# Short-sequence attention: 1 KB runs in DRAM, V reordered on TensorE, groups of 8 heads in three stages

## The chip, the core and the metric

The kernel runs on one core of a Trainium2 chip. The metric is device time in microseconds (us), the median of several runs. Beside those runs stands one profiled execution, from which every row below is taken. Engines: PE is TensorE (matmuls; PEld are its weight loads), DVE is VectorE, ACT is ScalarE, POOL is GpSimd, SP is SyncE. POOL issues the loads here and SP the stores; 16 DMA engines carry both. SBUF is the on-chip memory of 128 partitions, PSUM the memory of eight banks into which matmuls write.

## The reference

Attention for 32 batches of 12 heads, each with 128 tokens of 64 elements, no mask:

```python
scores = (1.0 / np.sqrt(64)) * np.matmul(q, k.transpose(0, 1, 3, 2))
attn = np.exp(scores - np.max(scores, axis=-1, keepdims=True))
attn = attn / (np.sum(attn, axis=-1, keepdims=True) + 1e-8)
return np.matmul(attn, v).astype(np.float32)
```

`q`, `k`, `v` and the result are float32 of shape (32, 12, 128, 64), 12.58 MB each. Both kernels compute in bf16 with float32 sums, leave the maximum out (the scores are small), and get the sum of each row of `attn` from a column of ones that stands beside V.

## The kernel before

The loop goes over the 32 batches. A batch is loaded by three DMAs on POOL's queue, which turn float32 into bf16 on the way (L52 q, L54 k, L57 v). A partition of SBUF holds one token, for all 12 heads, so that the runs in DRAM are the 64 floats of one token of one head: 256 B, and the same for the store. `v_bf` has 65 columns a head, the last set to one by a memset on POOL (L56). Input tiles have three buffers.

Then two heads at a time (`p` in 0 to 5): PE transposes 128 tokens x 128 elements of q into `qt_ps` (L63), ACT copies it to SBUF (L68), PE transposes the same of k into `kt_ps` (L70), DVE copies it (L75). `qt_ps` and `kt_ps` have one PSUM buffer each.

Then four heads at a time (`g` in 0 to 2): PE makes the four score matmuls into `sT_ps`, one bank a head (L84; a head's 64 elements lie in partitions 0 to 63 or 64 to 127, so neighbouring heads use the two halves of the array's rows). The scores come transposed, keys in the partitions. ACT takes the exp of all four (L92) into `attnT`. Two heads at a time, PE multiplies `attnT` with V and its ones into `o_ps` (L103), and DVE copies the two results to `o_b` (L110). `sT_ps` (four banks) and `o_ps` (two banks) have one buffer each.

At the end of a batch DVE takes the reciprocal of the 12 sums (L116), multiplies (L118), and SP issues the store (L119).

The instructions of an engine run in its own queue. The framework orders them by priority and by what is ready, within the buffers of each pool, and puts in the semaphores; a new tile of a pool waits until the reader of its old buffer has finished.

Of the kernel before, what the change touches and what calls it, by code (L numbers as in the profile page):

```python
# [1 line left out]

# [5 lines left out]


@with_exitstack
def kernel(
    ctx: ExitStack,
    tc: tile.TileContext,
    q: bass.AP,
    k: bass.AP,
    v: bass.AP,
    out: bass.AP,
):
    nc = tc.nc  # L20
    f32 = mybir.dt.float32
    bf16 = mybir.dt.bfloat16

    B, H, S, D = q.shape
    assert S == 128 and D == 64
    scale = 1.0 / (D ** 0.5)
    HT = 128 // D
    NP = H // HT
    HX = 4
    HO = 2  # L30
    BANK = 512

    qr = q.rearrange("b h s d -> b s h d")
    kr = k.rearrange("b h s d -> b s h d")
    vr = v.rearrange("b h s d -> b s h d")
    orr = out.rearrange("b h s d -> b s h d")

    singles = ctx.enter_context(tc.tile_pool(name="singles", bufs=1))
    ident = singles.tile([128, 128], bf16)
    make_identity(nc, ident)  # L40

    pbf = ctx.enter_context(tc.tile_pool(name="pbf", bufs=3))
    pt = ctx.enter_context(tc.tile_pool(name="pt", bufs=3))
    pa = ctx.enter_context(tc.tile_pool(name="pa", bufs=6))
    po = ctx.enter_context(tc.tile_pool(name="po", bufs=2))
    ps_t = ctx.enter_context(tc.tile_pool(name="ps_t", bufs=1, space=bass.MemoryType.PSUM))
    ps_s = ctx.enter_context(tc.tile_pool(name="ps_s", bufs=1, space=bass.MemoryType.PSUM))
    ps_o = ctx.enter_context(tc.tile_pool(name="ps_o", bufs=1, space=bass.MemoryType.PSUM))

    for b in range(B):  # L50
        q_bf = pbf.tile([128, H, D], bf16, tag="q_bf")
        nc.gpsimd.dma_start(out=q_bf, in_=qr[b])  # L52
        k_bf = pbf.tile([128, H, D], bf16, tag="k_bf")
        nc.gpsimd.dma_start(out=k_bf, in_=kr[b])  # L54
        v_bf = pbf.tile([128, H, D + 1], bf16, tag="v_bf")
        nc.gpsimd.memset(v_bf[:, :, D:D + 1], 1.0)  # L56
        nc.gpsimd.dma_start(out=v_bf[:, :, :D], in_=vr[b])  # L57

        qt = pt.tile([128, NP, 128], bf16, tag="qt")
        kt = pt.tile([128, NP, 128], bf16, tag="kt")  # L60
        for p in range(NP):
            qt_ps = ps_t.tile([128, 128], bf16, tag="qt_ps")
            nc.tensor.transpose(  # L63
                qt_ps,
                q_bf[:, p * HT:(p + 1) * HT, :].rearrange("a b c -> a (b c)"),
                ident,
            )
            nc.scalar.copy(qt[:, p, :], qt_ps)  # L68
            kt_ps = ps_t.tile([128, 128], bf16, tag="kt_ps")
            nc.tensor.transpose(  # L70
                kt_ps,
                k_bf[:, p * HT:(p + 1) * HT, :].rearrange("a b c -> a (b c)"),
                ident,
            )
            nc.vector.tensor_copy(kt[:, p, :], kt_ps)  # L75

        o_b = po.tile([128, H, D + 1], f32, tag="o_b")

        for g in range(H // HX):
            sT_ps = ps_s.tile([128, HX, BANK], f32, tag="sT")  # L80
            for i in range(HX):
                h = g * HX + i
                p, j = divmod(h, HT)
                nc.tensor.matmul(  # L84
                    sT_ps[:, i, :128],
                    lhsT=kt[j * D:(j + 1) * D, p, :],
                    rhs=qt[j * D:(j + 1) * D, p, :],
                    start=True,
                    stop=True,
                )  # L90
            attnT = pa.tile([128, HX, 128], bf16, tag="attnT")
            nc.scalar.activation(  # L92
                out=attnT,
                in_=sT_ps[:, :, :128],
                func=mybir.ActivationFunctionType.Exp,
                bias=0.0,
                scale=scale,
            )
            for gg in range(HX // HO):
                o_ps = ps_o.tile([128, HO, BANK], f32, tag="o_ps")  # L100
                for i in range(HO):
                    h = g * HX + gg * HO + i
                    nc.tensor.matmul(  # L103
                        o_ps[:, i, :D + 1],
                        lhsT=attnT[:, gg * HO + i, :],
                        rhs=v_bf[:, h, :],
                        start=True,
                        stop=True,
                    )
                nc.vector.tensor_copy(  # L110
                    o_b[:, g * HX + gg * HO:g * HX + (gg + 1) * HO, :],
                    o_ps[:, :, :D + 1],
                )

        recip = po.tile([128, H], f32, tag="recip")
        nc.vector.reciprocal(recip, o_b[:, :, D:D + 1])  # L116
        o_sb = po.tile([128, H, D], f32, tag="o_sb")
        nc.vector.tensor_mul(o_sb, o_b[:, :, :D], recip.to_broadcast([128, H, D]))  # L118
        nc.sync.dma_start(out=orr[b], in_=o_sb)  # L119


# [1 line left out]
_INS = ['q', 'k', 'v']  # L123
_OUTS = [((32, 12, 128, 64), 'float32')]


# [23 lines left out]
```

## Time and profile before

| | |
|---|---|
| time, median of 3 runs | 226.23 us (226.22 to 226.59) |
| span of the profiled execution | 224.4 us |
| PE busy | 168.3 us (75%), 1152 matmuls |
| PE weight loads busy | 83.1 us (37%), 1152 loads |
| DVE busy | 120.2 us (54%), 448 instructions |
| ACT busy | 99.7 us (44%), 289 instructions |
| POOL busy | 101.5 us (45%), 134 instructions |
| DMA packets | 198,674, of which 198,656 under 512 B |
| HBM traffic | 37.75 MB read, 12.58 MB written |

A row of groups reads: line, engine, operation, output <- input with shapes, count | busy us in total, mean ns of one | idle time of the engine just before them, and who ended it. A row of waits reads: who waited <- for whom: us in total, times, the longest. In the row of a stretch of time stand, after the stretch and its length, the busy time (and count) of PE, PEld, DVE, ACT and POOL, the granted clock of PE as a share, the summed time of packets as a share of 16 DMA engines, and GB/s. Packets of different queues overlap on an engine, so a sum of packet times can be over 100%. The bytes of a load count as they land, in bf16: half of what it reads.

### The profile page before, as it was taken

The page shows a single profiled execution, that of the slowest core. Times are in us where ns is not written, and L with a number is a line of the kernel's source. Part 1 is how long each engine was busy: PE and PEld are TensorE (multiplying, and loading weights), DVE is VectorE, ACT ScalarE, POOL GpSimd, SP SyncE. Part 2 cuts the span into 40 slices and gives each one's busy share as a digit, 9 for nine tenths or more (in the row PEclk, how much of TensorE's full clock was granted, in tenths as well). Part 3 has the DMA queues.
Part 4 walks back from the last instruction along what each step waited for, and adds up shares of the span by engine and source line. Part 5 has one row for each costly group of instructions (what it writes and reads, how often), then busy time and mean ns, then how long its engine had stood idle before and what let it go on. Part 6 is the DMA issues. An engine that isn't in the chain of part 4 may idle for free.

```text
span 224.4 us, 3513 instructions
## 1 busy us (share of the span) xinstructions
PE 168.3 (75%) x1152; PEld 83.1 (37%) x1152; DVE 120.2 (54%) x448; ACT 99.7 (44%) x289; POOL 101.5 (45%) x134
## 2 busy tenths in 40 slices
PE   0688787788787787877787877788877778878750
PEld 0344333344333343333343333444333334333330
DVE  0264555664555564555564555565555565456652
ACT  2554545445544445444445444444444444444320
POOL 8963455534475443455443455543355534222000
DMA  7999999999999999999999999999999999999333
GB/s 50 149 156 184 148 142 140 155 148 166 151 153 161 161 159 166 148 149 141 129 151 167 146 148 134 137 154 167 149 146 144 135 150 161 142 110 134 76 69 71
DMA packets 198674, 31.69 MB, mean 141 GB/s; under 512 B 198656, under 2 KB 198656, under 8 KB 198656
## 3 DMA queue, kind: packets, MB, share of 16 engines
q0 software_dynamic: 148992, 18.88, 131.9%
q1 hardware_dynamic: 49664, 12.58, 31.0%
q8 instruction: 9, 0.15, 0.3%
q14 instruction: 9, 0.07, 0.1%
HBM read 37.75 MB, written 12.58 MB: 224 GB/s over the span
## 4 chain that ended last, share of the span: by engine, by line
PE 64%; ACT 17%; DVE 9%; issue 6%; DMA 2%; ACTq 0%; POOL 0%; POOLq 0%
PE sT_ps L84 26%; PE qt_ps L63 14%; PE o_ps L103 14%; PE kt_ps L70 11%; ACT attnT L92 9%; ACT qt L68 7%; DVE o_b L110 5%; DVE kt L75 3%; DMA q_bf<-in_q_dram 2%; DVE o_sb L118 1%; ACTq L92 0%; DVE recip L116 0%; POOL ident masks.py:197 0%; POOLq masks.py:199 0%; POOLq L134 0%
## 5 line engine op out<-in xcount | busy, mean ns | idle before, releaser
L68 ACT COPY qt<-qt_ps 128x128 bf16<-128x128 bf16 x192 | 50.4, 263 | 69.0 <-PE qt_ps L63 69.0
L75 DVE COPY kt<-kt_ps 128x128 bf16<-128x128 bf16 x192 | 42.8, 223 | 70.8 <-PE kt_ps L70 66.1
L84 PE MATMUL sT_ps<-qt,kt 64*128 64x128 bf16 x384 | 71.5, 282 | 12.2 <-ACT attnT L92 11.5
L92 ACT ACTIVATE attnT<-sT_ps 128x512 bf16<-128x512 f32 x96 | 57.3, 597 | 47.7 <-PE sT_ps L84 42.9
L63 PE MATMUL qt_ps<-ident,q_bf 128*128 128x128 bf16 x192 | 54.2, 282 | 26.8 <-ACT qt L68 21.4
L110 DVE COPY o_b<-o_ps 128x130 f32<-128x130 f32 x192 | 55.6, 289 | 29.2 <-PE o_ps L103 28.9
L103 PE MATMUL o_ps<-v_bf,attnT 128*128 128x65 bf16 x384 | 56.8, 242 | 6.1 <-DVE o_b L110 6.1
L70 PE MATMUL kt_ps<-ident,k_bf 128*128 128x128 bf16 x192 | 56.4, 294 | 5.3 <-DVE kt L75 4.5
L84 PEld LDWEIGHTS <-kt 64*128 64x128 bf16 x384 | 26.4, 101 | 61.1 <-issue 43.0
L103 PEld LDWEIGHTS <-attnT 128*128 128x128 bf16 x384 | 34.3, 120 | 34.4 <-issue 26.5
L56 POOL MEMSET v_bf<- 128x12 bf16 x32 | 5.0, 155 | 79.9 <-PE o_ps L103 79.9
L52 POOL DMA_DIRECT2D q_bf<-in_q_dram x32 | 32.6, 1020 | 10.2 <-PE qt_ps L63 8.9
L57 POOL DMA_DIRECT2D v_bf<-in_v_dram x32 | 32.6, 1018 | 9.9 <-POOL v_bf L56 9.9
L54 POOL DMA_DIRECT2D k_bf<-in_k_dram x32 | 32.8, 1025 | 1.4 <-PE kt_ps L70 1.4
L63 PEld LDWEIGHTS <-q_bf 128*128 128x128 bf16 x192 | 18.9, 113 | 31.4 <-issue 15.7
L118 DVE TENSOR_TENSOR o_sb<-o_b,recip 128x768 f32<-128x768 f32 x32 | 30.3, 948 | 0.0
L70 PEld LDWEIGHTS <-k_bf 128*128 128x128 bf16 x192 | 23.2, 121 | 8.7 <-issue 0.9
L116 DVE RECIPROCAL recip<-o_b 128x12 f32<-128x12 f32 x32 | 7.0, 219 | 0.0
L68 ACT ACT_TABLE_LOAD x1 | 1.3, 1283 | 0.7 <-PEq L134 0.7
masks.py:199 POOL TENSOR_SCALAR_AFFINE_SELECT ident<-ident 128x128 bf16<-128x128 bf16 x1 | 0.3, 305 | 0.1
masks.py:197 POOL MEMSET ident<- 128x128 bf16 x1 | 0.2, 204 | 0.3 <-POOLq L134 0.3
L134 POOL MEMSET const-float32-0.0<- 128x1 f32 x1 | 0.1, 98 | 0.2 <-issue 0.2
(3 smaller groups left out, 0.3 us busy)
## 6 DMA issues: line engine op xcount, KB each, us to landing
out_dram<-o_sb SPq DMA_DIRECT2D x32, 384.0 KB, 5.7
q_bf<-in_q_dram POOLq DMA_DIRECT2D x32, 192.0 KB, 5.9
k_bf<-in_k_dram POOLq DMA_DIRECT2D x32, 192.0 KB, 6.4
v_bf<-in_v_dram POOLq DMA_DIRECT2D x32, 192.0 KB, 5.1
```

What stands on the lines that cost most here:

```text
L52: nc.gpsimd.dma_start(out=q_bf, in_=qr[b])
L54: nc.gpsimd.dma_start(out=k_bf, in_=kr[b])
L57: nc.gpsimd.dma_start(out=v_bf[:, :, :D], in_=vr[b])
L63: nc.tensor.transpose(qt_ps, q_bf[:, p * HT:(p + 1) * HT, :].rearrange("a b c -> a (b c)"), ident,)
L68: nc.scalar.copy(qt[:, p, :], qt_ps)
L70: nc.tensor.transpose(kt_ps, k_bf[:, p * HT:(p + 1) * HT, :].rearrange("a b c -> a (b c)"), ident,)
L75: nc.vector.tensor_copy(kt[:, p, :], kt_ps)
L84: nc.tensor.matmul(sT_ps[:, i, :128], lhsT=kt[j * D:(j + 1) * D, p, :], rhs=qt[j * D:(j + 1) * D, p, :], start=True, stop=True,)
L92: nc.scalar.activation(out=attnT, in_=sT_ps[:, :, :128], func=mybir.ActivationFunctionType.Exp, bias=0.0, scale=scale,)
L103: nc.tensor.matmul(o_ps[:, i, :D + 1], lhsT=attnT[:, gg * HO + i, :], rhs=v_bf[:, h, :], start=True, stop=True,)
L110: nc.vector.tensor_copy(o_b[:, g * HX + gg * HO:g * HX + (gg + 1) * HO, :], o_ps[:, :, :D + 1],)
L118: nc.vector.tensor_mul(o_sb, o_b[:, :, :D], recip.to_broadcast([128, H, D]))
```

## The change

DRAM is seen as blocks of 128 rows of 1 KB: a row is 4 tokens of one head, and a block is 4 heads (32 rows each). A chunk is 4 blocks (16 heads), loaded by three DMAs of the same kind as before; there are 24 chunks, each with SBUF tiles of its own, and all 72 loads are issued ahead of the compute. A partition holds 4 tokens (`t`) of one of 4 heads (`a`), and 32 partitions (`g`) make a head.

A group is two blocks, 8 heads; there are 48. The order of the work is that of the program text (a manual schedule), and the loop's step `s` does three stages of three groups:

- stage A of group `s`: 16 transposes, of q and k, for each of the 4 tokens and each of the 2 blocks, 128 partitions x 64 columns, the two blocks to the two halves of the PSUM partitions (column tiles of 64); one DVE copy of the whole `t_ps` to SBUF, which sorts by head; 16 matmuls with 32 columns of the identity, which bring V into an order with tokens in partitions, one token index `t` to each quarter of the PSUM partitions (column tiles of 32); one ACT copy into `v2`, whose ones were set once by DVE.
- stage B of group `s-1`: 8 score matmuls, one exp of 1024 columns on ACT.
- stage C of group `s-2`: 32 output matmuls, for each head and each token index, with 32 columns of `attn` as weights, one head to each quarter of the PSUM partitions (column tiles of 32); DVE takes the reciprocal out of PSUM and multiplies out of PSUM into `o_sb`; after every second group SP stores a chunk.

PSUM: `t_ps` and `v_ps` one bank each, `s_ps` two buffers of two banks, `o_ps` two banks.

```diff
-    qr = q.rearrange("b h s d -> b s h d")
+    T = 4
+    A = 4
+    G = S // T
+    NBLK = B * H // A
+    CB = 4
+    NCH = NBLK // CB
+    NG = NBLK // 2
+    GPC = CB // 2
+    def blocks(x):
+        return x.rearrange("b h (g t) d -> (b h g) (t d)", t=T).rearrange(
+            "(n p) x -> p n x", p=128)
+    qr, kr, vr, orr = blocks(q), blocks(k), blocks(v), blocks(out)
...
+    pin = ctx.enter_context(tc.tile_pool(name="pin", bufs=NCH))
+    pt = ctx.enter_context(tc.tile_pool(name="pt", bufs=3))
+    pa = ctx.enter_context(tc.tile_pool(name="pa", bufs=3))
+    po = ctx.enter_context(tc.tile_pool(name="po", bufs=4))
...
+    NV2 = 4
+    v2s = []
+    for i in range(NV2):
+        v2 = singles.tile([128, A, 2, D + 1], bf16, name=f"v2_{i}")
+        nc.vector.memset(v2[:, :, :, D:D + 1], 1.0)
+        v2s.append(v2)
+    def load(c):
+        sl = slice(c * CB, (c + 1) * CB)
+        tiles = []
+        for src, tag in ((qr, "q_bf"), (kr, "k_bf"), (vr, "v_bf")):
+            x = pin.tile([128, CB, T, D], bf16, tag=tag, name=tag)
+            nc.gpsimd.dma_start(out=x, in_=src[:, sl, :].rearrange("p n (t d) -> p n t d", t=T))
+            tiles.append(x)
+        chunks[c] = tiles
+    for c in range(NCH):
+        load(c)
+    with tc.manual_schedule():
...
+        def stage_a(i):
+            c, r = divmod(i, GPC)
+            q_bf, k_bf, v_bf = chunks[c]
+            bs = slice(2 * r, 2 * r + 2)
+            t_ps = ps_t.tile([128, T, 2, 128], bf16, tag="t_ps", name="t_ps")
+            for t in range(T):
+                for j, x in enumerate((q_bf, k_bf)):
+                    for b in range(2):
+                        nc.tensor.transpose(
+                            t_ps[b * D:(b + 1) * D, t, j, :], x[:, 2 * r + b, t, :], ident,
+                            tile_position=(0, b * D))
+            qkt = pt.tile([128, 2, A, T, G], bf16, tag="qkt", name="qkt")
+            nc.vector.tensor_copy(
+                qkt.rearrange("p j a t g -> p t (j a) g"),
+                t_ps.rearrange("p t j (a g) -> p t (j a) g", a=A))
+            qkts[i] = qkt
+            v_ps = ps_v.tile([128, A, 2, D], f32, tag="v_ps", name="v_ps")
+            for a in range(A):
+                for t in range(T):
+                    nc.tensor.matmul(
+                        v_ps[t * G:(t + 1) * G, a, :, :],
+                        lhsT=ident[:, a * G:(a + 1) * G],
+                        rhs=v_bf[:, bs, t, :],
+                        start=True, stop=True, tile_position=(0, t * G))
+            nc.scalar.copy(v2s[i % NV2][:, :, :, :D], v_ps)
+        def stage_b(i):
+            qkt = qkts.pop(i)
+            s_ps = ps_s.tile([128, 2, A, 128], f32, tag="s_ps", name="s_ps")
+            for a in range(A):
+                for j in range(2):
+                    pr = slice(j * D, (j + 1) * D)
+                    nc.tensor.matmul(
+                        s_ps[:, j, a, :],
+                        lhsT=qkt[pr, 1, a].rearrange("p t g -> p (t g)"),
+                        rhs=qkt[pr, 0, a].rearrange("p t g -> p (t g)"),
+                        start=True, stop=True)
+            attn = pa.tile([128, 2, A, 128], bf16, tag="attn", name="attn")
+            nc.scalar.activation(out=attn, in_=s_ps, func=mybir.ActivationFunctionType.Exp,
+                                 bias=0.0, scale=scale)
+            attns[i] = attn
+        def stage_c(i):
+            c, r = divmod(i, GPC)
+            attn = attns.pop(i)
+            v2 = v2s[i % NV2]
+            o_ps = ps_o.tile([128, 2, 512], f32, tag="o_ps", name="o_ps")
+            for j in range(2):
+                ov = o_ps[:, j, :T * (D + 1)].rearrange("p (t e) -> p t e", t=T)
+                for t in range(T):
+                    for a in range(A):
+                        nc.tensor.matmul(
+                            ov[a * G:(a + 1) * G, t, :],
+                            lhsT=attn[:, j, a, t * G:(t + 1) * G],
+                            rhs=v2[:, a, j, :],
+                            start=True, stop=True, tile_position=(0, a * G))
+            ov = o_ps[:, :, :T * (D + 1)].rearrange("p j (t e) -> p j t e", t=T)
+            if r == 0:
+                osbs[c] = po.tile([128, CB, T, D], f32, tag="o_sb", name="o_sb")
+            o_sb = osbs[c]
+            recip = pa.tile([128, 2, T], f32, tag="recip", name="recip")
+            nc.vector.reciprocal(recip, ov[:, :, :, D])
+            nc.vector.tensor_mul(o_sb[:, 2 * r:2 * r + 2], ov[:, :, :, :D],
+                                 recip.to_broadcast([128, 2, T, D]))
+            if r == GPC - 1:
+                nc.sync.dma_start(
+                    out=orr[:, c * CB:(c + 1) * CB, :],
+                    in_=o_sb.rearrange("p n t d -> p n (t d)"))
+                osbs.pop(c)
+        for s in range(NG + 2):
+            if s < NG:
+                stage_a(s)
+            if 0 <= s - 1 < NG:
+                stage_b(s - 1)
+            if 0 <= s - 2 < NG:
+                stage_c(s - 2)
```

More of the change, by code (lines that the diff above doesn't have):

```diff
@@ L26 @@
     scale = 1.0 / (D ** 0.5)
[L27 to L31, printed above, removed]
-    qr = q.rearrange("b h s d -> b s h d")
-    kr = k.rearrange("b h s d -> b s h d")
-    vr = v.rearrange("b h s d -> b s h d")
-    orr = out.rearrange("b h s d -> b s h d")
-    singles = ctx.enter_context(tc.tile_pool(name="singles", bufs=1))
+    T = 4
[9 more added lines that the diff above has]
+            "(n p) x -> p n x", p=128)
@@ L39 @@
+    ps_s = ctx.enter_context(tc.tile_pool(name="ps_s", bufs=2, space=bass.MemoryType.PSUM))
+    ps_o = ctx.enter_context(tc.tile_pool(name="ps_o", bufs=1, space=bass.MemoryType.PSUM))
     ident = singles.tile([128, 128], bf16)
     make_identity(nc, ident)
[L42 to L119, printed above, removed]
```

4 lines of the change are left out of this document (added).

## The prediction

> **What bounds the kernel now.** I read the page's head first, then the chain of waits by engine, the list of who waited for whom, the timeline at the start of a batch, and last the DMA rows.
>
> ```profile
> span 224.4 us, 3513 instructions
> PE 168.3 (75%) x1152; PEld 83.1 (37%) x1152; DVE 120.2 (54%) x448; ACT 99.7 (44%) x289; POOL 101.5 (45%) x134
> ...
> DMA  7999999999999999999999999999999999999333
> ...
> PE 64%; ACT 17%; DVE 9%; issue 6%; DMA 2%; ACTq 0%; POOL 0%; POOLq 0%
> ```
>
> The DMA row is at nine tenths nearly throughout, which looks like a memory bound, but DMA holds only 2% of the chain that ended last. PE, ACT and DVE share it, and none of them is full. The waits say why:
>
> ```profile
> POOL v_bf L56 <- PE o_ps L103: 79.9, 29, 4.2
> ACT qt L68 <- PE qt_ps L63: 69.0, 103, 3.6
> DVE kt L75 <- PE kt_ps L70: 66.1, 95, 7.6
> ...
> PE qt_ps L63 <- ACT qt L68: 21.4, 61, 0.4
> ```
>
> POOL, which issues the loads, waits 79.9 us for input buffers that PE has not finished with: loads are ahead of compute. ACT and DVE wait for PE's transposes, and PE waits for their copies. In the timeline (start, duration, in brackets the idle time and who ended it):
>
> ```profile
> 5.30 0.29 PE L63 MATMUL qt_ps<-ident,q_bf 128*128 128x128 bf16 x1 [5.30 <-DMA q_bf<-in_q_dram]
> 5.62 0.27 ACT L68 COPY qt<-qt_ps 128x128 bf16<-128x128 bf16 x1 [3.60 <-PE qt_ps L63]
> 5.94 0.27 PE L63 MATMUL qt_ps<-ident,q_bf 128*128 128x128 bf16 x1 [0.35 <-ACT qt L68]
> ```
>
> One transpose, one copy, one transpose: 0.64 us a turn, because `qt_ps` is one buffer. So the bound is a relay in small pieces through single PSUM buffers, and 12 heads cost about 224.4/32 = 7.0 us.
>
> **The change, part by part.** Work is regrouped into 48 groups of 8 heads, and a step of the new loop does stage A of one group, B of the group before and C of the one before that. What a step costs is the largest of five sums. I work out each.
>
> *DVE.* It loses 192 copies of `kt` and 192 of `o_b`, and gets per step one copy of 1024 bf16 elements out of PSUM, one reciprocal of 8, one multiply of 512 f32 elements that reads PSUM itself.
>
> ```profile
> L68 ACT COPY qt<-qt_ps 128x128 bf16<-128x128 bf16 x192 | 50.4, 263 | 69.0 <-PE qt_ps L63 69.0
> L75 DVE COPY kt<-kt_ps 128x128 bf16<-128x128 bf16 x192 | 42.8, 223 | 70.8 <-PE kt_ps L70 66.1
> ...
> L92 ACT ACTIVATE attnT<-sT_ps 128x512 bf16<-128x512 f32 x96 | 57.3, 597 | 47.7 <-PE sT_ps L84 42.9
> ...
> L110 DVE COPY o_b<-o_ps 128x130 f32<-128x130 f32 x192 | 55.6, 289 | 29.2 <-PE o_ps L103 28.9
> ...
> L118 DVE TENSOR_TENSOR o_sb<-o_b,recip 128x768 f32<-128x768 f32 x32 | 30.3, 948 | 0.0
> L116 DVE RECIPROCAL recip<-o_b 128x12 f32<-128x12 f32 x32 | 7.0, 219 | 0.0
> ```
>
> From 130 to 768 f32 elements the time grows by 659 ns, 1.03 ns an element over a fixed 155 ns. The bf16 copy of 128 takes 223 ns, so 0.53 an element. The new copy then takes 155 + 1024 x 0.53 = 0.70 us at the bf16 rate; in its runs of 32 it may fall to the f32 rate, 155 + 1024 x 1.03 = 1.21 us. The multiply is 155 + 512 x 1.03 = 0.68 us, the reciprocal at most 0.22. Sum 1.60 to 2.11 us.
>
> *ACT.* It loses the copies of `qt` and gets one copy of 512 and one exp of 1024. From 128 to 512 columns is 334 ns, 0.87 a column: 0.60 + (0.60 + 512 x 0.87 = 1.04) = 1.64 us.
>
> *PE.* A step has 72 matmuls: 16 transposes (A), 16 that reorder V (A), 8 for the scores (B), 32 for the output (C). Prices from the tiles' rows (min/median/max) and one burst:
>
> ```profile
> L63 PE MATMUL qt_ps<-ident,q_bf x192: 262/290/298, 5.3 to 204.7; 128*128 128x128 bf16 x192
> ...
> L103 PE MATMUL o_ps<-v_bf,attnT x384: 213/243/262, 10.6 to 218.5; 128*128 128x65 bf16 x192
> ```
>
> ```profile
> 11.20 0.40 PE L84 MATMUL sT_ps<-qt,kt 64*128 64x128 bf16 x4 [0.25 <-ACT attnT L92]
> 11.20 0.12 PEld L84 LDWEIGHTS <-kt 64*128 64x128 bf16 x3 [0.22 <-issue]
> ...
> 11.63 0.60 ACT L92 ACTIVATE attnT<-sT_ps 128x512 bf16<-128x512 f32 x1 [0.33 <-PE sT_ps L84]
> ```
>
> 128 columns against 65 cost 262 - 213 = 49 ns, 0.78 a column; so a matmul of 128 columns streams for 0.100 us, one of 65 for 0.051, and 0.162 is latency. Four score matmuls end 0.40 us after the first began. One after another they would need 0.162 + 4 x 0.100 = 0.56, two by two 0.36: the two halves of the rows run at once. Whether the new column tiles (two of 64 columns in the transposes, four of 32 in V and output) do so too no row shows. I take it that they do, since the rows that I have show it for halves. Then 16 x 0.100/2 + 16 x 0.100/4 + 8 x 0.100/2 + 32 x 0.051/4 = 0.80 + 0.40 + 0.40 + 0.41 = 2.0 us. The shape changes four times a step; if the array empties each time, 4 x 0.162 = 0.65 more: 2.65 us. With no overlap of column tiles it is 1.6 + 1.6 + 0.4 + 1.63 = 5.2 us. Ends 2.0 and 5.2 (5.9 with the emptying); I take 2.65.
>
> PE's waits go: `s_ps` has two buffers; the `t_ps` copy (0.70 to 1.21 us) lies under V, scores and outputs of the same step; `o_ps` is single, but the next group's outputs come only after its transposes, V and scores (1.6 us), longer than reciprocal and multiply (0.90). Without that cover the 0.90 would be on the path each step, 43 us in all.
>
> *DMA.* A descriptor's run in DRAM grows from 256 B to 1 KB, in loads and in stores.
>
> ```profile
> q0 software_dynamic: 148992, 18.88, 131.9%
> q1 hardware_dynamic: 49664, 12.58, 31.0%
> ...
> HBM read 37.75 MB, written 12.58 MB: 224 GB/s over the span
> ```
>
> ```profile
> 10.00:19.00 9.00, 7.41 (x57) 3.96 (x57) 4.67 (x19) 4.83 (x15) 6.05 (x8) 1.00 2.44 156
> ...
> 21.00:22.00 1.00, 0.83 (x9) 0.37 (x6) 0.69 (x3) 0.55 (x2) 0.36 (x2) 1.00 1.53 255
> ```
>
> The last column is GB/s as it arrives. From 10 to 19 us only loads run, none of them waiting for POOL (6.05 busy of 9): 156 GB/s of 127 B packets is 1.23 packets a ns, 13.0 ns a packet on each of 16 engines, and each fetches 256 B. After the change the loads are 37.75 MB / 1 KB = 36,864 packets and the stores 12,288: 2304 and 768 on each engine. A 1 KB packet costs at least 13 ns (all per packet) and at most 52 (all per byte). I take 42, three quarters of the way, since a transfer of four times the bytes is nearer to the byte price. Loads 2304 x 42 = 97 us, stores 32 us: 129 us in all, 2.69 a step. [...]
>
> *POOL.* 72 load issues instead of 96, and no 32 memsets.
>
> ```profile
> L52 POOL DMA_DIRECT2D q_bf<-in_q_dram x32 | 32.6, 1020 | 10.2 <-PE qt_ps L63 8.9
> ```
>
> 1.02 us each for 1536 runs; a new one has 512, so between 0.34 and 1.02 us, 24 to 73 us in all. Both lie under the 97 us of the transfers. No load waits for a buffer, as each chunk has its own. A full queue would stop POOL, but then transfers are queued already. SP's stores wait for the multiply; only later stores stand behind them.
>
> **The sum.** DMA 2.69 and PE 2.65 are nearly level; DVE and ACT lie under both.
>
> ```profile
> GB/s 50 149 156 184 148 142 140 155 148 166 151 153 161 161 159 166 148 149 141 129 151 167 146 148 134 137 154 167 149 146 144 135 150 161 142 110 134 76 69 71
> ```
>
> The first slice (5.61 us) moved 281 KB, 1.8 us at 156 GB/s: data flows from 3.8 us. By DMA: 3.8 + 97 + 22/24 of the 32 us of stores = 130.1 when the last load lands; then four steps that are no longer fed one by one, about 8 us (estimate: three times 2.65); then the last multiply (0.7) and the last store, from issue to end:
>
> ```profile
> 220.33 0.37 SPq L119 DMA_DIRECT2D out_dram<-o_sb  x1
> ```
>
> 224.4 - 220.3 = 4.1 us. Together 143 us. By PE: q and k of the first chunk are there at 3.8 + 2.7 + 1 = 7.5; then 48 steps of P, 1.7 P for the last two stages, 0.7 + 4.1 for multiply and store: 12.3 + 49.7 P, 144 us at P = 2.65. The profiled execution's 224.4 stands against a median of 226.2 us, 1.8 more, which I add: 145 and 146. I forecast **146 us**, its own range 136 to 160, since two nearly equal bounds disturb each other.
>
> **Rivals.**
> *Weight loads bind PE.* Now they are hidden: a transpose with its load right before takes 290 ns, with the load done earlier 262, so only 28 ns of a load's 106 show.
>
> ```profile
> L63 PEld LDWEIGHTS <-q_bf x192: 102/106/151, 5.3 to 204.0; 128*128 128x128 bf16 x192
> ```
>
> At 106/128 = 0.83 ns a column, one after another, with the scores' row halves in pairs: 16 x 0.053 + 16 x 0.027 + 4 x 0.106 + 32 x 0.027 = 2.56, with the emptying 3.2 us: 14.1 + 49.7 x 3.2 = 173 us. For it: there are 72 loads a step where 8 heads had 24; against: 28 of 106. [...]
> *A packet costs by its bytes* (52 ns): loads 120, stores 40, so 3.8 + 120 + 36.6 + 12.8 + 1.8 = 175 us. For it: the busiest stretch with stores carried 255 GB/s, no more. It is also the case that longer runs give nothing.
> *The column tiles run one after another*, and the time ends above the old one: P = 5.2, 14.1 + 49.7 x 5.2 = 273 us. It decides from P = (226.2 - 14.1)/49.7 = 4.27, when the 5.2 shrinks by less than a fifth. For it: three times as many matmuls, none of their overlap seen. Against: the row halves.
>
> **How the numbers follow.** The forecast has 0.50, weight loads 0.20, byte price 0.12, serial tiles 0.13; 0.05 is for both bounds being loose (PE at 2.0 and packets near 13 ns leave DVE's 2.11: 119 us). Range 132 to 195: it holds the first three, less their tails. A change of under 0.2% could not be told from none; faster by more than that 0.85, within it 0.01, slower 0.14.
>
> **What would show it.** Of the profile after: loads landing without a break, in packets of 512 B whose rate gives the 42 ns; the time from one step's exp to the next (2.7 us forecast; 3.2 or 5.2 by the rivals); four output matmuls beginning within a few ns and ending together; the DVE copy at 0.70 or 1.21; POOL without waits for PE. If PE rows fill the span with DMA idle behind, PE's price was wrong; if PE waits for `q_bf`, `k_bf` or `v_bf` in every chunk, the DMA bound was right.

## The result, and the profile after

The changed kernel takes 168.2 us (median of 4 runs, 167.0 to 170.6) where the kernel before took 226.3: a ratio of 0.741, 95% interval 0.738 to 0.745. (A ratio leaves out runs more than 1.5% above the fastest of their kernel, here the one of 170.6 us; the median has them in.) Forecast were 146 us, range 132 to 195. So the direction and the range held, and the central time was 22 us too low. The head, the clock, the DMA rows and the chain of the page after:

```profile
span 167.0 us, 7438 instructions
PE 108.6 (65%) x3456; PEld 80.4 (48%) x3456; DVE 74.4 (45%) x148; ACT 76.2 (46%) x97; POOL 54.1 (32%) x78
...
PE   0279619559558747686796576675595688878730
...
PEclk9999995876955895555567855696555899999985
DMA  3999999999999999999999999999999133333333
GB/s 45 141 195 198 192 226 202 237 209 231 231 208 241 197 242 237 201 241 198 223 218 242 218 222 240 197 244 222 214 235 219 46 129 134 129 129 129 129 129 126
...
q0 software_dynamic: 38016, 18.88, 84.3%
q1 hardware_dynamic: 12672, 12.58, 25.3%
q8 instruction: 27, 0.44, 1.0%
...
PE 38%; DMA 38%; issue 16%; DVE 3%; POOL 3%; POOLq 0%
```

The DMA row has two parts. Up to about 130 us (31 slices of 4.2 us) it is full; then the loads are in and 37 us follow with stores alone, one chunk's store at a time. PE is busy 68% of the time under the loads (30 to 130 us) and 78% after them (131 to 160 us). No compute engine is full, and "issue", time in which an engine waited for nothing that the profile shows, has 16% of the chain. The waits say whose time that is:

```profile
ACT v L103 <- PE v_ps L98: 76.7, 45, 8.3
DVE recip L140 <- PE o_ps L130: 64.7, 39, 4.2
...
PE o_ps L130 <- issue: 20.6, 13, 3.8
...
PE t_ps L87 <- issue: 8.1, 5, 2.5
PE v_ps L98 <- issue: 6.4, 4, 2.1
...
PE s_ps L111 <- issue: 6.0, 3, 3.3
```

ACT and DVE wait for PE, and PE's matmuls wait 41.1 us in 25 pieces for nothing visible. The timeline of one such piece:

```profile
81.67 0.24 PEld L130 LDWEIGHTS <-attn 128*32 128x32 bf16 x14 [0.20 <-issue]
81.67 0.40 PE L130 MATMUL o_ps<-v,attn 128*32 128x65 bf16 x14
...
82.94 0.30 PEld L130 LDWEIGHTS <-attn 128*32 128x32 bf16 x18 [1.03 <-issue]
82.94 0.46 PE L130 MATMUL o_ps<-v,attn 128*32 128x65 bf16 x18 [0.87 <-issue]
```

The 32 output matmuls of a group depend on the same two tiles, which are there when the first begins; yet PE stops after 14 of them. Other breaks fall into the transposes, the V matmuls or the scores, wherever PE happens to be. Four breaks in a row under loads, then three after the loads:

```profile
44.40 0.22 PE L87 MATMUL t_ps<-ident,k_bf 128*64 128x128 bf16 x1 [2.08 <-issue]
...
50.78 0.30 PE L130 MATMUL o_ps<-v,attn 128*32 128x65 bf16 x6 [2.43 <-issue]
...
57.23 0.37 PE L130 MATMUL o_ps<-v,attn 128*32 128x65 bf16 x23 [1.20 <-issue]
...
63.71 0.50 PE L111 MATMUL s_ps<-qkt 64*128 64x128 bf16 x6 [3.34 <-issue]
...
140.60 0.24 PE L98 MATMUL v_ps<-v_bf,ident 128*32 128x128 bf16 x3 [0.46 <-issue]
...
144.17 0.25 PE L87 MATMUL t_ps<-ident,q_bf 128*64 128x128 bf16 x2 [0.47 <-issue]
...
148.02 0.22 PE L130 MATMUL o_ps<-v,attn 128*32 128x65 bf16 x5 [0.96 <-issue]
```

They are 6.4 us apart under loads and 3.6 to 3.9 after them, and in the trace 254 or 255 matmuls and weight loads lie between one and the next, every time. The queue named "instruction" (q8) moved 27 packets, 0.44 MB, 16 KB each. 27 x 256 = 6912 is the number of PE's matmuls and weight loads, so a packet holds 256 of them, at 64 B. In the kernel before PE had 2304, a third, and that queue moved 9 packets.

The times of these packets tie the two together. In the trace each of the 25 breaks between 18.5 and 155.9 us ends 2.2 to 2.8 us after such a packet began to move, and a packet moves for about 1 us, with loads and without. The next packet begins 3.7 to 4.5 us after PE went on while loads run (3.1 the one time that they ended meanwhile), and 1.1 to 1.7 us after it once they are in. So what the loads lengthen is the wait before the packet moves.

### The profile page after: what moved, and what is told of

The parts are those of the page before. It is cut to its first block, busy times and chain, and to the rows that moved or that the text cites. A ratio compares the mean times of both kernels' runs of the same rounds, so it can differ in the third digit from the quotient of the medians.

```text
span 167.0 us, 7438 instructions
## 1 busy us (share of the span) xinstructions
PE 108.6 (65%) x3456; PEld 80.4 (48%) x3456; DVE 74.4 (45%) x148; ACT 76.2 (46%) x97; POOL 54.1 (32%) x78
## 2 busy tenths in 40 slices
DMA packets 50718, 31.93 MB, mean 191 GB/s; under 512 B 1536, under 2 KB 50688, under 8 KB 50688
## 3 DMA queue, kind: packets, MB, share of 16 engines
q0 software_dynamic: 38016, 18.88, 84.3%
## 4 chain that ended last, share of the span: by engine, by line
PE 38%; DMA 38%; issue 16%; DVE 3%; POOL 3%; POOLq 0%
DMA k_bf<-in_k_dram 16%; PE t_ps L87 13%; DMA v_bf<-in_v_dram 13%; PE o_ps L130 10%; DMA q_bf<-in_q_dram 9%; PE v_ps L98 8%; PE s_ps L111 7%; DVE o_sb L141 2%; POOL q_bf L69 1%; POOL k_bf L69 1%; DVE qkt L91 1%; DVE recip L140 1%; POOL v_bf L69 0%; POOL ident masks.py:199 0%; POOL ident masks.py:197 0%
## 5 line engine op out<-in xcount | busy, mean ns | idle before, releaser
L103 ACT CAST v<-v_ps 128x512 bf16<-128x512 f32 x48 | 28.2, 587 | 76.9 <-PE v_ps L98 76.7
L117 ACT ACTIVATE attn<-s_ps 128x1024 bf16<-128x1024 f32 x48 | 49.1, 1026 | 6.2 <-PE s_ps L111 6.2
L87 PE MATMUL t_ps<-ident,q_bf 128*64 128x128 bf16 x384 | 38.7, 274 | 7.6 <-DMA q_bf<-in_q_dram 5.1
L87 PE MATMUL t_ps<-ident,k_bf 128*64 128x128 bf16 x384 | 38.4, 271 | 8.0 <-issue 5.9
L130 PE MATMUL o_ps<-v,attn 128*32 128x65 bf16 x1536 | 27.9, 218 | 22.5 <-issue 20.6
L91 DVE COPY qkt<-t_ps 128x1024 bf16<-128x1024 bf16 x48 | 33.0, 687 | 20.6 <-PE t_ps L87 19.7
L87 PEld LDWEIGHTS <-q_bf 128*64 128x64 bf16 x384 | 27.1, 139 | 16.5 <-issue 8.1
L141 DVE TENSOR_TENSOR o_sb<-o_ps,recip 128x512 f32<-128x512 f32 x48 | 33.2, 691 | 1.9 <-DVE recip L140 0.3
L98 PE MATMUL v_ps<-v_bf,ident 128*32 128x128 bf16 x768 | 25.3, 263 | 9.5 <-issue 6.4
L87 PEld LDWEIGHTS <-k_bf 128*64 128x64 bf16 x384 | 28.2, 143 | 3.7 <-DMA k_bf<-in_k_dram 2.3
```

What stands on the lines that cost most here:

```text
L87: nc.tensor.transpose(t_ps[b * D:(b + 1) * D, t, j, :], x[:, 2 * r + b, t, :], ident, tile_position=(0, b * D))
L91: nc.vector.tensor_copy(qkt.rearrange("p j a t g -> p t (j a) g"), t_ps.rearrange("p t j (a g) -> p t (j a) g", a=A))
L98: nc.tensor.matmul(v_ps[t * G:(t + 1) * G, a, :, :], lhsT=ident[:, a * G:(a + 1) * G], rhs=v_bf[:, bs, t, :], start=True, stop=True, tile_ ...
L103: nc.scalar.copy(v2s[i % NV2][:, :, :, :D], v_ps)
L117: nc.scalar.activation(out=attn, in_=s_ps, func=mybir.ActivationFunctionType.Exp, bias=0.0, scale=scale)
L130: nc.tensor.matmul(ov[a * G:(a + 1) * G, t, :], lhsT=attn[:, j, a, t * G:(t + 1) * G], rhs=v2[:, a, j, :], start=True, stop=True, tile_pos ...
```

## The experiments

Three theories, used in the expectations below. **F**: PE waits for its own instructions, which arrive in blocks of 256, and a block takes a round trip that is 6.4 us long beside loads. **M**: PE's work itself (72 matmuls a step, the clock) sets the time, and the breaks only stand where PE would have waited anyway. **R**: the transfers are the bound.

**The transfers alone.** All compute is left out; loads and stores stay.

```diff
-    with tc.manual_schedule(): ...
+    o_sb = po.tile([128, CB, T, D], f32, tag="o_sb", name="o_sb")
+    nc.vector.memset(o_sb, 0.5)
+    for c in range(NCH):
+        nc.sync.dma_start(
+            out=orr[:, c * CB:(c + 1) * CB, :],
+            in_=o_sb.rearrange("p n t d -> p n (t d)"))
```

> Leaves out all compute: the 72 loads and the 24 stores of the changed kernel alone, the stores from a constant tile. Theory F (the changed kernel waits for PE's instructions, which come in blocks of 256 behind the load traffic) and theory M (PE is too slow for its 72 matmuls a step) both expect the transfers themselves to be cheap: 2304 packets at 41 ns and 768 at 41 ns on each engine, 94 + 31 us, with the start 130 to 137 us in all. Theory R (the transfers are the bound, since DMA holds 38% of the chain in the changed kernel) expects nearly the time of the changed kernel, 160 us or more.

And the same with runs of 256 B, as the kernel before has them:

```diff
-    qr, kr, vr, orr = blocks(q), blocks(k), blocks(v), blocks(out)
+    qr, kr, vr, orr = (x.rearrange("b h s d -> s (b h) d") for x in (q, k, v, out))
...
+            x = pin.tile([128, CB * A, D], bf16, tag=tag, name=tag)
+            nc.gpsimd.dma_start(out=x, in_=src[:, c * CB * A:(c + 1) * CB * A, :])
```

> Leaves out all compute: the same bytes as loads and stores, but in the layout of before (runs of 256 B). At 13.0 ns a packet: loads 9216 x 13.0 = 120 us, stores 3072 x 14 = 43 us, with the start 165 to 175 us. If a packet cost by its bytes alone this would equal the run with 1 KB runs (130 to 137 us). F, M and R do not differ here; it gives what the longer runs are worth by themselves.

Measured, one run each: 145.8 us with 1 KB runs, 206.9 us with 256 B. The first lies between F's and M's 130 to 137 and R's 160 or more, the second 32 us above the 165 to 175 of all three. The stretches of the first show why (after the length stand DVE, POOL, the clock, the packets' time as a share of 16 engines, and GB/s; stores run from the start to 79 us here, then loads alone):

```profile
20.00:70.00 50.00, 0.00 (x0) 12.58 (x17) 1.00 1.25 258
90.00:130.00 40.00, 0.00 (x0) 22.22 (x30) 1.00 1.45 196
```

Loads alone: 196 GB/s of 497 B packets (18.88 MB / 38,016) is 0.394 packets a ns, 40.6 ns on each of 16 engines (41.8 if the 1152 packets of 4 B among them are left out). Loads and stores together go packet for packet (in the trace 692 and 693 from 30 to 34 us), 497 and 993 B, so 258 GB/s is 0.346 packets a ns, 46.2 ns each. In this run the mixture cost 14% more a packet than loads alone. R falls: 146 us is 22 us under the changed kernel. The second run gives what the change's longer runs are worth by themselves, 61 us off the floor, and puts the kernel before only 20 us above its own floor.

**No loads beside the compute.** Only chunk 0 is loaded; every group computes from it.

```diff
-    for c in range(NCH):
-        load(c)
+    load(0)
+    for c in range(1, NCH):
+        chunks[c] = chunks[0]
```

> Loads chunk 0 only and computes every group from it, so the output is that of chunk 0 throughout; PE's instructions, DVE, ACT and the stores are as in the changed kernel. F: a block of 256 PE instructions takes the 3.7 us that it takes in the changed kernel after its loads have ended, 27 blocks in all, 100 to 115 us. M: PE at the half-speed price of 2.64 us a step, 48 steps and 12 us, 139 us, or the changed kernel's time less little. R: as fast as compute goes, no number of its own, but no PE pauses every 256 instructions.

Measured, one run: 122.9 us. M's 139 is refuted, F's 100 to 115 is missed by 8 us. Head and clock of that page:

```profile
span 121.1 us, 7366 instructions
PE 88.4 (73%) x3456; PEld 67.1 (55%) x3456; DVE 72.9 (60%) x148; ACT 74.4 (61%) x97; POOL 3.0 (2%) x9
...
PEclk9999999999999999967999999997699999999985
```

The same 27 instruction packets arrive 4.0 us apart in the trace (6.4 under loads); the breaks are still there, 254 or 255 instructions apart or a multiple of that, and end 2.2 to 2.8 us after a packet began; but they are short, and PE mostly has full clock. M's 139 was worked out at half clock; with the 1.72 us that a step takes at full clock (shown at the end) it would be some 95 us, an estimate (48 x 1.72 + 12), 28 below the measured time. So M is out as the whole story at either clock, but this run took away the load traffic with the fetch's delay, so it does not separate F from R by itself. The next two change little but the number of instructions.

**Fewer PE instructions for the same columns.** V of a whole chunk is reordered at once, in matmuls of 256 columns. For room in PSUM the scores have one buffer; that part alone is its own run. ACT's 48 copies of V become 24 of twice the size.

```diff
-    ps_s = ctx.enter_context(tc.tile_pool(name="ps_s", bufs=2, ...))
+    ps_s = ctx.enter_context(tc.tile_pool(name="ps_s", bufs=1, ...))
...
+            if r == 0:
+                v_ps = ps_v.tile([128, A, CB, D], f32, tag="v_ps", name="v_ps")
...
-                        rhs=v_bf[:, bs, t, :],
+                        rhs=v_bf[:, :, t, :],
```

> V is reordered for a whole chunk at once, 16 matmuls of 256 columns for two groups in place of 32 of 128: the same columns stream through PE, the same bytes move, but PE has 6144 instructions in place of 6912, 24 blocks of 256 in place of 27 (the scores have one PSUM buffer, to make room). F: three blocks fewer at the 3.7 us of the stretch without loads, or at 6.4 under loads: 11 to 19 us less than the changed kernel's 168, 149 to 158 us. M (PE's streaming sets the time): no change, 165 to 170 us. R (transfers): no change, 165 to 170 us.

> The changed kernel with one PSUM buffer for the scores in place of two, and nothing else: what the run with merged V gave up for its room. F, M and R: the next scores come a step later than the exp that frees the buffer (1.03 us), so no change, 166 to 171 us. If the second buffer mattered, each step would wait up to 0.5 us: up to 190 us.

**More PE instructions for the same columns.**

```diff
-                    nc.tensor.matmul(
-                        v_ps[t * G:(t + 1) * G, a, :, :], ...
-                        rhs=v_bf[:, bs, t, :],
+                    for b in range(2):
+                        nc.tensor.matmul(
+                            v_ps[t * G:(t + 1) * G, a, b, :], ...
+                            rhs=v_bf[:, 2 * r + b, t, :],
```

> The other way round from the merged V: V is reordered by 32 matmuls of 64 columns a step in place of 16 of 128. Same columns, same bytes, but 8448 PE instructions, 33 blocks of 256 in place of 27. F: six blocks more, at 3.75 us (after the loads) to 6.4: 190 to 207 us. M and R: 168 to 172 us, since the columns that stream and the transfers are the same.

Measured: 160.6 us with 6144 instructions (ratio to the kernel before 0.708, interval 0.707 to 0.710), 168.2 with one score buffer alone and 187.1 with 8448 (one run each). M and R expected no change from either; F has the sign of both. Its sizes were too large: 7.6 us less for three blocks (expected 11 to 19), 18.9 more for six (expected 22 to 38). The trace has the reason. Under loads the interval stays 6.4 to 6.5 us in all three, so blocks are won or lost in the stretch after the loads, at 3.8 to 4.2 us each on average; and when compute is slower, fewer stores mix with the loads (12, 15 and 18 are done by their end), and these end sooner: at 125 us with 8448 instructions, 130 with 6912, 136 with 6144. An estimate from these figures: loads that end 5.5 us sooner cover 0.9 block less, so six blocks more cost 6.9 x 3.8 - 5.5 = 21 us; three fewer save 9 by the same working.

The times alone would also fit a fixed price of an instruction, 12 ns in one run (18.9 us for 1536) and 10 in the other (7.6 for 768). The breaks speak against it: in both runs they come every 254 to 256 instructions or a multiple of that and end 2.2 to 2.8 us after an instruction packet began, as in the changed kernel. And PE's waits for nothing visible add up to 57.1 us with 8448 instructions, 41.1 with 6912 and 29.5 with 6144.

**What makes a block slow under loads.** Loads issued only three chunks ahead, or in halves:

```diff
-    pin = ctx.enter_context(tc.tile_pool(name="pin", bufs=NCH))
+    pin = ctx.enter_context(tc.tile_pool(name="pin", bufs=4))
...
-    for c in range(NCH):
+    for c in range(3):
         load(c)
...
+            if s % GPC == 0 and s // GPC + 3 < NCH:
+                load(s // GPC + 3)
```

> A chunk's loads are issued only when the buffer of four chunks before is free (4 buffers a tensor in place of 24), so that the load queue holds at most three chunks. F, if a fetch of PE's instructions is slow because a long queue of loads stands ahead of it: blocks nearer to 4 us than 6.4, 145 to 160 us. F, if it is slow because the transfer engines are busy at all: as before, 165 to 172 us, since three chunks ahead still fill the queue. R: loads come later, 170 us or more.

```diff
-            nc.gpsimd.dma_start(out=x, in_=src[:, sl, :].rearrange("p n (t d) -> p n t d", t=T))
+            w = CB // 2
+            for y in range(0, CB, w):
+                nc.gpsimd.dma_start(
+                    out=x[:, y:y + w],
+                    in_=src[:, c * CB + y:c * CB + y + w, :].rearrange("p n (t d) -> p n t d", t=T))
```

> Each load DMA is split into two of half the size, 16 packets of 1 KB on each engine in place of 32; the rest is as in the changed kernel. F, if a fetch waits for its turn behind whole load DMAs on its engine (2.7 us more than without loads, about two DMAs of 32 packets at 41 ns): the wait halves, 5.1 us a block under loads, 148 to 160 us. F, if the size of a DMA does not matter for the turn: 166 to 171 us. R: no change, 166 to 171 us; POOL issues 144 loads of some 0.7 us, 100 us, still ahead of the transfers.

Measured: 169.8 us paced (ratio 0.743, interval 0.739 to 0.748, no different from the changed kernel's), 162.4 in halves (0.715, 0.712 to 0.717). Pacing left the interval at 6.4 us in the median, with three chunks issued ahead in place of 24. Halves bring it to 5.5 us in the median (3.8 to 8.2), where 3.6 to 3.9 would be the interval without loads: a third of what loads add. What shrinks is the wait before the packet moves, from about 4.0 us to a median of 3.1. So the size of a load DMA enters the wait of a fetch; by what turn-taking on the engine the runs do not show.

**Both, and V without PE.** Merged V with loads in halves:

> Merged V and loads in halves together. F: 24 blocks at 5.5 us under loads, so both gains (7.6 and 5.8 us) should nearly add up: 152 to 157 us. If the transfers already bind the merged kernel (146 us for loads and stores alone), the second gain shrinks: 157 to 161 us. M and R: no reason for a gain over 160.6 us.

Measured: 156.5 us, ratio 0.690 (0.688 to 0.691), the fastest version, 11.7 us under the changed kernel. The gains nearly add (7.6 + 5.8 = 13.4). One of its waits and its chain:

```profile
PE v_ps L103 <- DMA v_bf<-in_v_dram: 25.4, 20, 2.7
...
DMA 58%; POOL 29%; issue 5%; PE 2%; ACT 2%; DVE 1%; POOLq 0%; ACTq 0%
```

PE has 2% of the chain. Its matmuls still wait for nothing visible, but 7.5 us where the changed kernel's wait 41.1; in 20 of the 24 chunks V's matmuls wait for their load instead. The transfers and their issue on POOL (144 loads in place of 72) hold the time now, 11 us above the transfers' own 146; what POOL's part alone is worth no run shows.

The other loads V with tokens in partitions, in 256 B runs, and drops V's matmuls; ACT takes over the copy of the keys:

```diff
+        nc.gpsimd.dma_start(out=x[:, :, :D], in_=vhr[:, c * CB * A:(c + 1) * CB * A, :])
...
+            nc.scalar.copy(
+                kt.rearrange("p a (g t) -> p a g t", t=T),
+                k_ps[:, :T, :].rearrange("p t (a g) -> p a g t", a=A))
...
-                        rhs=v2[:, a, j, :],
+                        rhs=v_bf[:, (2 * r + j) * A + a, :],
```

> V is not reordered on PE at all: it is loaded with tokens in partitions, in runs of 256 B, and the keys are brought into the same order by the copy of their transposes, which ACT takes over from DVE (q stays with DVE). 5376 PE instructions, 21 blocks. F: 21 blocks at 6.4 us under loads would be 134 us with the first two free, under the transfers: those rise by V's 49,152 packets of 256 B at 13 ns in place of 12,288 at 41 ns, 9 us more than the 146 us of transfers alone, 153 to 162 us. M: PE loses 0.55 us of 2.64 a step, 26 us, so 142 to 152 us. R: 168 + 9 = 177 us.

Measured: 161.3 us (0.712, 0.711 to 0.713), within F's 153 to 162 and outside M's and R's numbers; DMA has 79% of its chain. With 21 blocks it is no faster than merged V alone with 24 (160.6): fewer instructions brought nothing more here, with V in packets of 256 B.

**Undoing the placed outputs.** Outputs by 8 matmuls of 128 columns of weights, q read in steps for the scores, stores in 256 B runs:

```diff
-                        rhs=qkt[pr, 0, a].rearrange("p t g -> p (t g)"),
+                        rhs=qkt[pr, 0, a].rearrange("p t g -> p g t"),
...
-                            ov[a * G:(a + 1) * G, t, :],
-                            lhsT=attn[:, j, a, t * G:(t + 1) * G],
-                            rhs=v2[:, a, j, :],
-                            start=True, stop=True, tile_position=(0, a * G))
...
+                        ov[:, a, :],
+                        lhsT=attn[:, j, a, :],
+                        rhs=v2[:, a, j, :],
+                        start=True, stop=True)
...
+                    out=ohr[:, c * CB * A:(c + 1) * CB * A, :],
```

> Undoes the outputs by 32-column tiles: 8 output matmuls of 128 columns of weights a step in place of 32, the result with tokens in partitions and stores in runs of 256 B. PE instructions fall from 6912 to 4608, 18 blocks in place of 27. F: 16 + 16 blocks x 6.4 = 118 us would do for the instructions, so the transfers bind: loads 94 us, stores 3072 x 13 = 40 us, start and end 15 us, 145 to 158 us. M: the 8 matmuls stream as long as the 32 did (8 x 65 columns against 32 x 65 on four tiles at once), so the time stays within 3%, 163 to 170 us. R: the stores get dearer by 8 us, 170 us or more.

Measured: 188.5 us (ratio 0.831, 0.830 to 0.833). F's and M's numbers failed; R's "170 us or more", for dearer stores, held. There were 18 blocks, as F said, and none of PE's matmuls waits for nothing visible any more: its breaks come every 192 instructions (two steps), at no fixed time after a packet. Another wait came first.

```profile
DVE o_sb L141 <- DMA out_dram<-o_sb: 40.3, 12, 4.5
...
L112 PE MATMUL s_ps<-qkt x384: 372/390/393, 12.6 to 179.5; 64*128 64x128 bf16 x192
```

DVE waits 40.3 us for its output buffers. The stores go in 256 B packets here, and the queues took turns packet by packet (in the trace 4843 of the loads and 4845 of the stores from 40 to 60 us), so a store got a fraction of the bytes beside 1 KB loads: it landed in 19.9 us where the changed kernel's took 7.6. The scores also got slower, 390 ns in the median with q read in steps where the longest of the changed kernel took 311, so this run mixes three things: fewer matmuls, smaller stores, slower scores. All in all the placed outputs are worth 20 us; how much of that is their 1 KB stores the run does not show.

## Why the prediction was right in range and low by 22 us

*Right, with their measures.* The DVE, ACT and DMA prices:

```profile
L103 ACT CAST v<-v_ps 128x512 bf16<-128x512 f32 x48 | 28.2, 587 | 76.9 <-PE v_ps L98 76.7
L117 ACT ACTIVATE attn<-s_ps 128x1024 bf16<-128x1024 f32 x48 | 49.1, 1026 | 6.2 <-PE s_ps L111 6.2
...
L91 DVE COPY qkt<-t_ps 128x1024 bf16<-128x1024 bf16 x48 | 33.0, 687 | 20.6 <-PE t_ps L87 19.7
...
L141 DVE TENSOR_TENSOR o_sb<-o_ps,recip 128x512 f32<-128x512 f32 x48 | 33.2, 691 | 1.9 <-DVE recip L140 0.3
...
L69 POOL DMA_DIRECT2D k_bf<-in_k_dram x24 | 17.9, 746 | 22.2 <-DMA v_bf<-in_v_dram 22.2
```

The large copy took 0.69 us (0.70 at the bf16 rate), the multiply 0.69 (0.68), ACT 1.61 a step (1.64), a load's issue on POOL 0.75 (0.34 to 1.02). POOL waited 62 us between its issues, 62 times, until earlier loads had landed, with a buffer for each load: the stop that the prediction allowed for, and the DMA row stays at nine tenths meanwhile. A load's 1 KB packet took 40.6 ns with loads alone where I took 42, an estimate between 13 and 52 (196 GB/s from 10 to 18 us in the changed kernel's trace, and the same in the run of the transfers alone; the 41 ns of the expectations agrees with it). The byte-price rival (52 ns) is refuted.

*Right: the price of a step on PE.* From the first transpose of one step to that of the next, where no break falls between:

```profile
83.34 0.32 PE L87 MATMUL t_ps<-ident,q_bf 128*64 128x128 bf16 x2
...
84.33 0.62 PE L98 MATMUL v_ps<-v_bf,ident 128*32 128x128 bf16 x16
...
84.88 0.61 PE L111 MATMUL s_ps<-qkt 64*128 64x128 bf16 x8
...
85.42 0.63 PE L130 MATMUL o_ps<-v,attn 128*32 128x65 bf16 x32
...
85.98 0.32 PE L87 MATMUL t_ps<-ident,q_bf 128*64 128x128 bf16 x2
```

2.64 us, forecast 2.65; and its four parts, 0.99, 0.55, 0.54 and 0.56, are the forecast's 0.96, 0.56, 0.56 and 0.57 (with 0.16 for each change of shape). That is the price at half clock, to which the rows of the kernel before are near; at full clock the step takes 1.72, which the prediction does not know. Sixteen V matmuls of 128 columns are done in 0.62 us; one after another they would stream for 1.6. So column tiles run at once, and the rival that was slower than before fell at its premise. The weight-load rival (3.2 us a step; 173 us) came near the measured time for the wrong reason: the step of 2.64 has no room for them, so weight loads stay hidden.

*Wrong: the step "What a step costs is the largest of five sums", with "PE's waits go".* PE's waits on tiles went, as argued: 1.8 us on `o_ps` are left, where 43 were the price without cover. A sixth sum was missing, PE's supply of instructions: 144 a step, 256 in 6.4 us, so 3.6 us a step under loads and 2.1 after them, where DMA needs 2.7 and PE 2.65 or less. Over the run the steps are 3.17 us apart, by the 48 copies from 8.5 to 157.6 us (47 intervals):

```profile
L91 DVE COPY qkt<-t_ps x48: 680/691/692, 8.5 to 157.6; 128x1024 bf16<-128x1024 bf16 x48
```

The prediction had asked for three times the matmuls and priced their columns, the changes of shape and, as a rival, their weight loads, but not the delivery of the instructions. It is shown that the time follows the number of instructions with columns and bytes unchanged (two runs, both directions), that each break ends 2.2 to 2.8 us after a block began to move, and that a block takes longer beside loads (6.4 us against 3.6 to 3.9).

*Luck: the range.* The measured time is outside the forecast's own range (136 to 160). The wide one, 132 to 195, holds it only because it was drawn around the weight-load and byte-price rivals, at 173 and 175 us, and both of these are false.

*Right by accident: the last load's landing.* Forecast 130.1 us, with 22 of 24 stores done; the trace has it at 130.2, with 15. The missing stores (7 x 1.33 = 9.3 us) are made up for by the mixing cost, which I had at nothing (some 5.4 us, an estimate: 480 packets of stores on each engine beside as many of loads, 5.6 ns more each), and by a rest that stays open. The 12.8 us after it (four steps, the last multiply and store) became 37, since compute was that far behind.

*Missed on the kernel before.* It was read as loads well ahead of compute. So they were, but the transfers alone, with all loads issued ahead, need 207 us in runs of 256 B: with those runs the rest of the change could hardly have gained more than a tenth.

## What to carry to other kernels

Count the instructions of each engine, not only their work: here small tiles made 144 PE instructions for every 2.7 us of transfers, the supply of 256 in 6.4 us beside loads was the bound, and it showed as waits for nothing, 254 or 255 instructions apart, in the middle of work that depends on nothing new. Widen the moving operand where PSUM has room (here 16 matmuls of 256 columns for 32 of 128, 7.6 us), and measure the transfers alone to know what is left.

## What the runs showed of the hardware

*PE's instructions came in blocks of 256.* 27 packets of 16 KB stand beside 6912 matmuls and weight loads in the changed kernel, 9 beside 2304 in the kernel before. The cost was not hidden here: PE's matmuls waited 41.1 us of 167 for nothing visible, with one block in 6.4 us beside loads, 5.5 beside loads of half the size and 3.6 to 4.0 without loads.

*The two busy DMA queues took turns packet by packet*, also where the runs differ in size (692 to 693 with loads and stores of 1 KB runs, in the transfers alone; 4843 to 4845 with stores of 256 B, in the run with the outputs undone), and with loads and stores mixed a 1 KB packet took 46.2 ns in place of 40.6 (in the transfers alone).

*The granted clock goes to half, and the breaks do not explain it.* At the granted half clock (the 5s in the clock row) a pair of transposes takes 0.31 us in the changed kernel, at full clock 0.22, and the step without a break falls from 2.64 us to 1.72 (from 156.57 to 158.29 in the trace). The changed kernel has half clock mostly under loads, where its breaks are long (a mean granted clock of 0.65 from 30 to 130 us, 1.00 from 131 to 160). But in the run with the outputs undone PE has no break of over 0.3 us between 10.5 and 68 us, and its transposes take half clock's time there and nearly throughout (min, median and max in ns):

```profile
L88 PE MATMUL t_ps<-ident,q_bf x384: 219/313/317, 5.2 to 176.4; 128*64 128x128 bf16 x192
```

What sets the clock stays open. The kernel before shows a clock of 1.000 throughout, but its transposes of as many columns took 262 to 290 ns: its trace has no clock record at all, and its durations are nearer to those at half clock. So here the matmuls tell more of the clock than the row does.
